# First projections on unnormalised tokens, with a larger pool of raw weight buffers

## The chip, the cores and the metric

The kernel runs on one core of one Trainium2 chip. The metric is the device time of one execution in microseconds (us). PE is the matrix engine, DVE VectorE, ACT ScalarE, POOL GpSimd, SP the engine whose queue issues all the transfers here.

## What is computed

A two-layer encoder over 256 tokens of width 1024, all in fp32. Each layer normalises the tokens, sends them through one wide input projection whose columns feed three mixers (latent attention, convolution, retention) and gates, merges the branches, and adds a normalised result to the tokens; a feed-forward part follows. The part that the change touches is the beginning of layer 0:

```
def rms_norm(x, g):
    y = xf * lax.rsqrt(jnp.mean(xf * xf, -1, keepdims=True) + EPS)
    return y * g
...
    for l in range(DEPTH):
        h = rms_norm(x, ln_mix_pre[l])
        proj = h @ w_in[l]
        c_q, c_kv, k_pe, conv_u, r_q, r_k, r_v, r_g, gate_logits = jnp.split(proj, points, axis=-1)
```

The row factor of the norm is one number for each token and the gain one number for each of the 1024 inputs, so `(x * rs * g) @ w` equals `rs * (x @ (g * w))`. In c_q, c_kv and k_pe (416 columns) lie the latents and the rotary key; r_v are 1024 columns, of which the first 512 are made at the start.

## The kernel before

Tokens lie in two blocks of 128 (b = 0, 1), the 1024 inputs in eight tiles of 128. Every fp32 product is made of three: operands are split into a high part (fp32r) and a low remainder, and high x high, high x low and low x high are summed in a PSUM bank.

**Weights.** `wunit` (L171) takes one unit of 1024 columns a partition: SP transfers it to a raw buffer (tag raw, NRAW = 5 of them), ACT casts it to whi (L175, 9 buffers), DVE subtracts to wlo (L177, 8 buffers). A raw buffer is free when its subtraction is done, and only then may SP issue the transfer that reuses it. SP issues in program order; each transfer also waits for the one eight places ahead of it. `split` (L182, L183) does cast and subtraction for activations.

**Front.** SP brings the gain row (4 KB) and then token block 0. PE runs warm-up matmuls (L128) and spreads the gain row over the partitions by a matmul with ones (L131). `first_norm` (L293) squares a block on ACT and DVE; POOL makes rs (L142, L143); DVE makes hn = x * rs * g (L278); PE transposes hn (L284); `split` writes hT, high and low. Then `behind` multiplies hT by the latents' weights ua (416 columns) and the value weights uv (512): L205 for the products with hT's high part, L208 for those with its low part.

**Behind the front.** `setup_tables` makes sinT, cosT, sinq, cosq from the positions (DVE, then one Sin each on ACT, L365) and the decay constants lg of the retention (27 small DVE operations and one on ACT, L374 to L387). `latent` norms the latents of a block (squares on ACT L457, L458; POOL; DVE L462, L464) and applies the rotary factors to the key (kpad, L392 to L397); later PE transposes cn (L474) and kpad (L475), and ACT copies them to cT and kT. Meanwhile PE runs feature groups, `feat_group` with `mm3` (L186 to L188), for the convolution's inputs; two units of weights each, 24 products for each half j.

**Boundaries.** `boundary` joins two sub-layers, three times in all: the new tokens of block 0 are normed and transposed (L284) while PE still works on block 1's last products, ACT casts hT, and the next sub-layer's products begin.

The order inside an engine is the scheduler's: the program is recorded, and instructions are moved past each other where the data allow it. Loops over units set it only roughly.

## Time and profile before

| | |
|---|---|
| time, median of 3 runs (lowest to highest) | 934.63 us (933.78 to 935.09) |
| the profiled execution, its span | 934.14 us, 932.1 us |
| PE busy | 924.0 us (99%), 4924 matmuls |
| PE weight loads, beside the matmuls | 787.0 us (84%) |
| DVE busy | 694.0 us (74%) |
| ACT busy | 534.6 us (57%) |
| POOL busy | 36.8 us (4%) |
| moved from memory | 164.80 MB, 178 GB/s over the span |

The busy share says how full an engine was over the whole span. The chain says which engine's work, followed back from the end, set it. Busy PE time is modelled and pipelined: a row's duration has a tail that lies under the next row, so the cost of one matmul in a run of equal ones is the distance of their starts. The page's clock row shows the full level over all slices, since records begin with the rise; the level before that is read from the same distances.

### The profile page before, as it was taken

The page shows a single profiled execution, that of the slowest core. Times are in us where ns is not written, and L with a number is a line of the kernel's source. Part 1 is how long each engine was busy: PE and PEld are TensorE (multiplying, and loading weights), DVE is VectorE, ACT ScalarE, POOL GpSimd, SP SyncE. Part 2 cuts the span into 40 slices and gives each one's busy share as a digit, 9 for nine tenths or more (in the row PEclk, how much of TensorE's full clock was granted, in tenths as well). Part 3 has the DMA queues.
Part 4 walks back from the last instruction along what each step waited for, and adds up shares of the span by engine and source line. Part 5 has one row for each costly group of instructions (what it writes and reads, how often), then busy time and mean ns, then how long its engine had stood idle before and what let it go on. Part 6 is the DMA issues. An engine that isn't in the chain of part 4 may idle for free.

```text
span 932.1 us, 13291 instructions
## 1 busy us (share of the span) xinstructions
PE 924.0 (99%) x4924; PEld 787.0 (84%) x4924; DVE 694.0 (74%) x1101; ACT 534.6 (57%) x821; POOL 36.8 (4%) x77
## 2 busy tenths in 40 slices
PE   9999999999999999999999999999999999999997
PEld 6999878888888888888889987788888888888885
DVE  7889999996657766664485899999766677676532
ACT  5774886545545665554365758755454556666421
POOL 2000000000010000000120000010000100000000
PEclk9999999999999999999999999999999999999999
DMA  6885454566636766666376656545665376665621
GB/s 226 250 271 162 139 174 163 154 191 182 193 91 229 248 193 191 189 194 193 102 213 201 182 156 178 183 136 163 197 181 180 126 230 204 186 182 189 201 83 45
DMA packets 113214, 166.70 MB, mean 179 GB/s; under 512 B 5929, under 2 KB 62905, under 8 KB 113150
## 3 DMA queue, kind: packets, MB, share of 16 engines
q1 hardware_dynamic: 113150, 165.87, 58.6%
q8 instruction: 38, 0.62, 0.3%
q14 instruction: 26, 0.21, 0.1%
HBM read 164.80 MB, written 1.05 MB: 178 GB/s over the span
## 4 chain that ended last, share of the span: by engine, by line
PE 97%; DMA 1%; ACT 1%; DVE 0%; SPq 0%; issue 0%; DVEq 0%; POOLq 0%; POOL 0%; ACTq 0%
PE acc L186 20%; PE acc L187 19%; PE acc L188 19%; PE acc L255 13%; PE acc L253 7%; PE acc L205 6%; PE acc L208 3%; PE acc L252 2%; PE tp L627 1%; PE tp L663 1%; PE tp L652 1%; DMA raw<-in_w_in_dram 1%; PE tp L693 1%; PE tp L284 1%; PE tp L187 1%; PE tp L188 1%
## 5 line engine op out<-in xcount | busy, mean ns | idle before, releaser
L177 DVE TENSOR_TENSOR wlo<-raw,whi 128x1024 fp32r<-128x1024 f32 (+1 forms) x300 | 363.3, 1218 | 103.8 <-PE acc L187 58.9
L175 ACT CAST whi<-raw 128x1024 fp32r<-128x1024 f32 (+1 forms) x300 | 312.6, 1049 | 222.8 <-PE acc L188 122.1
L255 PE MATMUL acc<-hT,whi 128*128 128x512 f32 x504 | 179.7, 396 | 0.0
L253 PE MATMUL acc<-hT,wlo 128*128 128x256 f32 x576 | 148.9, 279 | 0.0
L186 PE MATMUL acc<-whi,hT 128*128 128x512 f32 x288 | 118.1, 410 | 0.0
L253 PEld LDWEIGHTS acc<-hT,wlo 128*128 128x128 f32 x576 | 108.6, 189 | 6.2
L187 PE MATMUL acc<-wlo,hT 128*128 128x512 f32 x288 | 112.7, 391 | 0.0
L188 PE MATMUL acc<-whi,hT 128*128 128x512 f32 x288 | 112.5, 391 | 0.0
L255 PEld LDWEIGHTS acc<-hT,whi 128*128 128x128 f32 x504 | 94.6, 188 | 19.5
L535 DVE SCALAR_TENSOR_TENSOR cacc<-apad,ccol,cacc 128x256 f32<-128x256 f32 x240 | 108.8, 482 | 1.3
L186 PE MATMUL acc<-hT,whi 128*128 128x256 f32 x256 | 73.2, 286 | 0.0
L188 PE MATMUL acc<-hT,wlo 128*128 128x256 f32 x256 | 72.4, 283 | 0.0
L187 PE MATMUL acc<-hT,whi 128*128 128x256 f32 x256 | 72.4, 283 | 0.0
L186 PE MATMUL acc<-whi,hidh 128*128 128x512 f32 x176 | 68.6, 390 | 0.0
L187 PE MATMUL acc<-wlo,hidh 128*128 128x512 f32 x176 | 68.5, 389 | 0.0
L188 PE MATMUL acc<-whi,hidl 128*128 128x512 f32 x176 | 68.5, 389 | 0.0
L186 PEld LDWEIGHTS acc<-whi,hT 128*128 128x128 f32 x288 | 54.1, 188 | 13.4 <-issue 3.1
L188 PEld LDWEIGHTS acc<-whi,hT 128*128 128x128 f32 x288 | 54.1, 188 | 12.1
L187 PEld LDWEIGHTS acc<-wlo,hT 128*128 128x128 f32 x288 | 54.2, 188 | 10.2
L205 PE MATMUL acc<-whi,hT 128*128 128x512 f32 (+1 forms) x128 | 49.4, 387 | 0.5 <-ACT hT L182 0.4
L186 PEld LDWEIGHTS acc<-hT,whi 128*128 128x128 f32 x256 | 49.1, 192 | 0.2
L187 PEld LDWEIGHTS acc<-hT,whi 128*128 128x128 f32 x256 | 49.1, 192 | 0.2
(248 smaller groups left out, 1478.6 us busy)
## 6 DMA issues: line engine op xcount, KB each, us to landing
raw<-in_w_in_dram SPq DMA_DIRECT2D x112, 512.0 KB, 4.3
raw<-in_ffn_w_gate_dram SPq DMA_DIRECT2D x44, 512.0 KB, 4.3
raw<-in_ffn_w_up_dram SPq DMA_DIRECT2D x44, 512.0 KB, 4.5
raw<-in_ffn_w_down_dram SPq DMA_DIRECT2D x44, 512.0 KB, 4.5
raw<-in_ret_w_o_dram SPq DMA_DIRECT2D x16, 512.0 KB, 3.5
raw<-in_w_out_dram SPq DMA_DIRECT2D x16, 512.0 KB, 3.6
raw<-in_mla_w_o_dram SPq DMA_DIRECT2D x8, 512.0 KB, 4.7
raw<-in_conv_w_pw_dram SPq DMA_DIRECT2D x8, 512.0 KB, 3.6
```

Of the source, the lines that this page charges most:

```text
L175: S.copy(hi, raw)
L177: V.tensor_sub(lo, raw, hi.bitcast(F32))
L186: T.matmul(o, lh, rh, start=start, stop=False)
L187: T.matmul(o, lh, rl, start=False, stop=False)
L188: T.matmul(o, ll, rh, start=False, stop=stop)
L205: T.matmul(o, ah[:, 2 * i + k, :], w[:, k, :], start=not (i or k or n), stop=False)
L208: T.matmul(o, al[:, 2 * i - 2 + k, :], units[i - 1][0][:, k, :], start=False, stop=i == len(units) and k == 1)
L252: T.matmul(ps, wh, both[:, k, :], start=True, stop=False)
L253: T.matmul(ps[:, SEQ:], wl, both[:, k, :SEQ], start=False, stop=False)
L255: T.matmul(ps, wh, both[:, k, :], start=False, stop=k == KT - 1)
L284: T.transpose(ps[:, j * P:(j + 1) * P], hn[:, (4 * c + j) * P:(4 * c + j + 1) * P], ident)
L535: V.scalar_tensor_tensor(cacc[:, j, :], src, ccol[:, j, w:w + 1], cacc[:, j, :], op0=ALU.mult, op1=ALU.add)
```

## The change

For layer 0 alone, the latents' group and the value group multiply the tokens as they come. PE transposes the raw tokens (`plain_T`), `split` writes uTh and uTl; the gain is put on the weights while they are split (`scaled_unit`, a factor for each partition from pcol, a transposed 8 x 128 gain tile), and the row factor rs on the results (sa for the latents, vrh and vrl for the values). The squares stand behind the latents' weights on ACT and DVE. The normalised hT, which all later groups need, is still made, between the value products. The gain comes as a 512 KB broadcast. A chain (`Line`) fixes the order of the front's instructions on PE, ACT and DVE. NRAW goes from 5 to 7; the warm-ups from 10 to 7 and one; the positions' transfers are issued ahead of the value weights; the decay constants are made behind the rotary queries.

```
-NRAW = 5
-WARM = 10
+NRAW = 7
+WARM = 7
...
-    nc.sync.dma_start(grow1[0:1, :], ln_mix_pre[0:1, :])
     nc.sync.dma_start(xs[:, 0, :], x[0, 0:P, :])
...
+    g8 = act.tile([KT, P], F32, tag="grow", name="g8")
+    nc.sync.dma_start(g8, ln_mix_pre[0].rearrange("(k p) -> k p", p=P))
...
-    for i in range(WARM):
-        T.matmul(pw, warm[:, :P], warm, start=True, stop=True)
-        if i == 3:
-            for c in range(2):
-                T.matmul(gfirst[c], ones, grow1[0:1, c * 512:(c + 1) * 512], start=True, stop=True)
+    keep_busy(WARM)
...
+    def plain_T(b, c, u):
+        ps = tp()
+        for j in range(4):
+            inPE(T.transpose(ps[:, j * P:(j + 1) * P], xs[:, b, (4 * c + j) * P:(4 * c + j + 1) * P], ident))
+        hi, lo = (t[:, 4 * c:4 * c + 4, b * P:(b + 1) * P] for t in u)
+        pv = ps.rearrange("p (j n) -> p j n", j=4)
+        inACT(S.copy(hi, pv))
+        return lambda: inDVE(V.tensor_sub(lo, pv, hi.bitcast(F32)))
+
+    def scaled_unit(src, k0, c, col):
+        raw = wraw(src, 2, c)[:, :2 * c].rearrange("p (k c) -> p k c", k=2)
+        hi, lo = (t[:, :2 * c].rearrange("p (k c) -> p k c", k=2) for t in (hi_tile(), lo_tile()))
+        for k in range(2):
+            inACT(S.activation(hi[:, k, :], raw[:, k, :], AF.Copy, scale=col[:, k0 + k:k0 + k + 1]))
+        for k in range(2):
+            inDVE(V.scalar_tensor_tensor(lo[:, k, :], raw[:, k, :], col[:, k0 + k:k0 + k + 1],
+                                         hi[:, k, :].bitcast(F32), op0=ALU.mult, op1=ALU.subtract))
...
-        S.activation(hn[:, :512], xs[:, b, :512], AF.Square, scale=1.0 / 32.0, accum_out=ss[:, 0:1])
-        V.scalar_tensor_tensor(hn[:, 512:], xs[:, b, 512:], 1.0 / D, xs[:, b, 512:],
-                               op0=ALU.mult, op1=ALU.mult, accum_out=ss[:, 1:2])
-        pre_norm(b, hn, ss, gain, hT)()
+        inACT(S.activation(hn[:, :512], xs[:, b, :512], AF.Square, scale=1.0 / 32.0, accum_out=ss[:, 0:1]))
+        inDVE(V.scalar_tensor_tensor(hn[:, 512:], xs[:, b, 512:], 1.0 / D, xs[:, b, 512:],
+                                     op0=ALU.mult, op1=ALU.mult, accum_out=ss[:, 1:2]))
...
+        lo = plain_T(0, 0, u)
+        lo()
+        unit(0)
+        lo = plain_T(0, 1, u)
+        lo()
+        nc.sync.dma_start(xs[:, 1, :], x[0, P:2 * P, :])
+        keep_busy(1)
+        products(0, 0, "hh")
+        products(0, 0, "lh")
+        for c in range(2):
+            plain_T(1, c, u)()
+        products(0, 0, "hl")
...
+            uT, pcol = fast_first(pas)
+            tables = load_tables()
+            gain = gain_tile(ln_mix_pre[0])
+            squares = [first_squares(b) for b in range(NB)]
+            uv, first = [], []
+            for i in range(4):
+                uv.append(scaled_unit(win[2 * i * P:(2 * i + 2) * P, C_RV:C_RV + 512], 2 * i, 512, pcol))
+                if i < NB:
+                    first.append(pre_norm(i, *squares[i], [gain[:, cs] for cs in halves()], hT, inDVE))
...
+            for b in range(NB):
+                sa = half("sa")[:, :C_CONV]
+                S.activation(sa, pas[b][:, :C_CONV], AF.Copy, scale=first[b].rs)
+                pas[b] = sa
+            for i in range(4):
+                for b in range(NB):
+                    tok_mm(pvs[b], uT, b, 2 * i, uv[i], 2, i == 0, i == 3)
+                if i in (1, 2):
+                    first[i - 1]()
+            for b in range(NB):
+                vh, vl = vrh[:, b, :512], vrl[:, b, :512]
+                S.activation(vh, pvs[b], AF.Copy, scale=first[b].rs)
+                V.scalar_tensor_tensor(vl, pvs[b], first[b].rs, vh.bitcast(F32), op0=ALU.mult, op1=ALU.subtract)
...
+        if l == 0:
+            setup_decays()
```

On PE, at the rotary keys: cn are the normed latents, kpad the rotary keys, the products are those of the feature groups. Before, the first transpose of kpad stands 12 products behind block 0's cn, the second right behind block 1's, in the middle of a group:

```order
L474 MATMUL tp_541<-ident_96,cn_406 128x128 x3
L475 MATMUL tp_541<-ident_96,kpad_109 96x128
L186 MATMUL acc_516<-hT_111,whi_506 128x256
L187 MATMUL acc_516<-hT_111,whi_506 128x256
L188 MATMUL acc_516<-hT_111,wlo_508 128x256
```

And after, 24 products behind block 1's cn, where the next group begins:

```order
L197 MATMUL acc_536<-hT_102,whi_532 128x256
L198 MATMUL acc_536<-hT_102,wlo_534 128x256
L559 MATMUL tp_516<-ident_87,kpad_100 96x128
L196 MATMUL acc_607<-hT_102,whi_597 128x256
L559 MATMUL tp_561<-ident_87,kpad_100 96x128
L197 MATMUL acc_607<-hT_102,whi_597 128x256
L198 MATMUL acc_607<-hT_102,wlo_599 128x256
```

Both transposes of kpad have moved behind the whole second group, around the first product of the third.

On ACT, at the sine tables: whi of 256 and 128 columns are the query weights, of 1024 the feature weights, th the convolution's gate. Before:

```order
L182 CAST vrh<-acc 128x512
L365 ACT_TABLE_LOAD
L365 ACTIVATE sinT<-sinT 128x288
L175 CAST whi<-raw 128x1024 x3
L182 CAST vrh<-acc 128x512
L175 CAST whi<-raw 128x1024 x3
L365 ACTIVATE cosT<-cosT 128x288
L175 CAST whi<-raw 128x1024
L522 ACT_TABLE_LOAD
L522 ACTIVATE th<-acc 128x512
```

And after:

```order
L541 ACTIVATE cn_426,ss2_427<-sa_300 128x256
L542 ACTIVATE cn_426,ss2_427<-sa_300 128x128
L192 CAST whi_726<-raw_724 128x256
L192 CAST whi_722<-raw_724 128x128
L396 ACT_TABLE_LOAD
L396 ACTIVATE sinT_95<-sinT_95 128x288
L192 CAST whi_726<-raw_724 128x256
L192 CAST whi_722<-raw_724 128x128
L192 CAST whi_738<-raw_736 128x256
L192 CAST whi_722<-raw_736 128x128
L618 ACT_TABLE_LOAD
L618 ACTIVATE th_444<-acc_457 128x512
```

The sine has moved behind both blocks' latents and the first query weights, and the gate now stands between sine and cosine (two casts, a table load and the cosine follow), so the tables are loaded twice more.

On ACT, at the first boundary (junk: squares of the banks; hn: squares of the new tokens; whi: weights of the next sub-layer). Before:

```order
L314 ACTIVATE hn,ss_2810<-xs 128x512 x2
L175 CAST whi<-raw 128x1024 x2
L305 ACTIVATE junk,ss_2885<-acc 128x512
L175 CAST whi<-raw 128x1024 x3
L182 CAST hT<-tp 128x4x128 x2
```

And after:

```order
L347 ACTIVATE hn,ss_2858<-xs 128x512 x2
L185 CAST whi<-raw 128x1024 x2
L338 ACTIVATE junk,ss_2933<-acc 128x512
L185 CAST whi<-raw 128x1024 x4
L192 CAST hT<-tp 128x4x128 x2
```

One more weight cast stands ahead of hT's; it is the same at the other two boundaries.

## Rows read from the trace of the kernel before

**Rows 1.** The page, chain that ended last: each engine's share of the span

```profile
PE 97%; DMA 1%; ACT 1%; DVE 0%; SPq 0%; issue 0%; DVEq 0%; POOLq 0%; POOL 0%; ACTq 0%
```

**Rows 2.** Timeline of PE: start and duration (us), line, operation, [idle before <-releaser]

```profile
4.39 3.78 PE L131 MATMUL acc<-grow,ones 1*128 1x512 f32 x4
...
9.36 1.91 PE L284 MATMUL tp<-ident,hn 128*128 128x128 f32 x8
...
11.46 0.72 PE L205 MATMUL acc<-whi,hT 128*128 128x416 f32 x1 [0.19 <-ACT hT L182]
...
12.32 0.55 PE L205 MATMUL acc<-whi,hT 128*128 128x416 f32 x1
12.66 0.47 PE L205 MATMUL acc<-wlo,hT 128*128 128x416 f32 x1
12.97 0.35 PE L205 MATMUL acc<-whi,hT 128*128 128x416 f32 x1
13.16 0.35 PE L205 MATMUL acc<-wlo,hT 128*128 128x416 f32 x1
```

**Rows 3.** Timeline of ScalarE, at the front and at one later boundary

```profile
4.97 0.63 ACT L293 ACTIVATE hn<-xs 128x512 f32<-128x512 f32 x1 [2.97 <-DMA xs<-in_x_dram]
...
5.98 0.88 ACT L175 CAST whi<-raw 128x832 fp32r<-128x832 f32 x1 [0.29 <-DMA raw<-in_w_in_dram]
...
28.88 1.28 ACT L365 ACT_TABLE_LOAD   x1
...
42.07 0.90 ACT L182 CAST whi<-raw 128x256 fp32r<-128x256 f32 x3
...
282.56 1.06 ACT L175 CAST whi<-raw 128x1024 fp32r<-128x1024 f32 x1 [1.19 <-PE tp L284]
```

**Rows 4.** Timeline of SP's queue: issue and duration, transfer

```profile
1.13 0.35 SPq L120 DMA_DIRECT2D xs<-in_x_dram  x1
...
37.03 2.57 SPq L166 DMA_DIRECT2D raw<-in_mla_w_uq_dram  x2
```

**Rows 5.** Timeline of PE: second transposes, last value products, two feature pairs

```profile
14.86 0.60 PE L284 MATMUL tp<-ident,hn 128*128 128x128 f32 x4
...
32.14 1.07 PE L208 MATMUL acc<-whi,hT 128*128 128x512 f32 x4
33.05 0.28 PE L186 MATMUL acc<-hT,whi 128*128 128x256 f32 x1
...
46.12 0.28 PE L186 MATMUL acc<-hT,whi 128*128 128x256 f32 x1
```

**Rows 6.** Timeline of VectorE, from the second norm past kpad

```profile
13.13 1.39 DVE L278 SCALAR_TENSOR_TENSOR hn<-xs,rs,acc 128x512 f32<-128x512 f32 x2
...
21.12 0.16 DVE L348 CAST pos<-pos_i 128x2 f32<-128x2 int32 x1
...
22.53 0.39 DVE L354 TENSOR_SCALAR ang<-inv,pos 128x16 f32<-128x16 f32 x2 [0.67 <-DMA inv<-in_inv_row_dram]
...
25.12 0.17 DVE L374 TENSOR_SCALAR lgt<-lgt 128x16 f32<-128x16 f32 x1 [1.86 <-DMA lgt<-in_ret_decay_logits_dram]
...
40.00 0.17 DVE L384 TENSOR_SCALAR lgt<-lgt 128x16 f32<-128x16 f32 x1
...
40.17 0.17 DVE L397 TENSOR_TENSOR kpad<-kpad,tk 128x16 f32<-128x16 f32 x1
...
44.99 2.35 DVE L177 TENSOR_TENSOR wlo<-raw,whi 128x1024 fp32r<-128x1024 f32 x2
```

**Rows 7.** Groups by line and shape, Pool, first 60 us: busy us, mean ns

```profile
L139 POOL TENSOR_TENSOR rs<-rs,nhalf 128x2 f32<-128x2 f32 x2 | 1.5, 738 | 0.2
```

**Rows 8.** Timeline of PE at two boundaries between sub-layers

```profile
283.55 0.40 PE L188 MATMUL acc<-whi,mTl 128*128 128x512 f32 x1
284.15 0.50 PE L205 MATMUL acc<-whi,hT 128*128 128x512 f32 x1 [0.20 <-ACT hT L182]
...
740.80 0.40 PE L188 MATMUL acc<-whi,mTl 128*128 128x512 f32 x1
741.27 0.50 PE L205 MATMUL acc<-whi,hT 128*128 128x512 f32 x1
```

More of the change, by code (lines that the diff above doesn't have):

```diff
@@ L117, in tile_hybrid_encoder, with __init__, __call__ @@
     xs = cst.tile([P, NB, D], F32, tag="xs", name="xs")
-    grow1 = mid("grow1")
-    nc.sync.dma_start(grow1[0:1, :], ln_mix_pre[0:1, :])
     nc.sync.dma_start(xs[:, 0, :], x[0, 0:P, :])
-    ones = cst.tile([1, P], F32, tag="ones", name="ones")
-    V.memset(ones, 1.0)
+    g8 = act.tile([KT, P], F32, tag="grow", name="g8")
+    nc.sync.dma_start(g8, ln_mix_pre[0].rearrange("(k p) -> k p", p=P))
+    class Line:
+        def __init__(self):
+            self.last = None
+        def __call__(self, ins):
+            if self.last is not None:
+                tc.add_manual_dep(ins.ins, self.last, mybir.DependencyInfo(
+                    mybir.DependencyClass.NoSync, mybir.DependencyReason.DATA), reason="order")
+            self.last = ins.ins.name
+    inPE, inACT, inDVE = Line(), Line(), Line()
     warm = act.tile([P, 512], BF16, tag="half", name="warm", bufs=7)
@@ L125, in tile_hybrid_encoder, with keep_busy @@
     pw = tp()
-    gfirst = [acc() for _ in range(2)]
-    for i in range(WARM):
-        T.matmul(pw, warm[:, :P], warm, start=True, stop=True)
-        if i == 3:
-            for c in range(2):
-                T.matmul(gfirst[c], ones, grow1[0:1, c * 512:(c + 1) * 512], start=True, stop=True)
+    def keep_busy(n):
+        for _ in range(n):
+            inPE(T.matmul(pw, warm[:, :P], warm, start=True, stop=True))
+    keep_busy(WARM)
     ident = cst.tile([P, P], F32, tag="ident", name="ident")
@@ L272, in new_hT, with pre_norm @@
         return t[:, :, :SEQ], t[:, :, SEQ:]
-    def pre_norm(b, hn, ss, gain, hT):
+    def pre_norm(b, hn, ss, gain, hT, line=lambda ins: None):
         rs = sm.tile([P, 1], F32, tag="rs", name="rs")
@@ L277, in pre_norm @@
         for c, cs in enumerate(halves()):
-            V.scalar_tensor_tensor(hn[:, cs], xs[:, b, cs], rs, gain[c], op0=ALU.mult, op1=ALU.mult)
+            line(V.scalar_tensor_tensor(hn[:, cs], xs[:, b, cs], rs, gain[c], op0=ALU.mult, op1=ALU.mult))
         def transposes():
@@ L368, in setup_tables, with setup_decays @@
         V.tensor_scalar(sinq, sinr, sc, None, op0=ALU.mult)
+    def setup_decays():
+        lgt = half("lgt")
+        n = DEPTH * 2 * RH
+        xl = lgt[:, 0:n]
+        nc.sync.dma_start(xl, ret_decay_logits.rearrange("l t h -> (l t h)").partition_broadcast(P))
+        nc.sync.dma_start(relt, rel)
         u = lgt[:, 16:32]
@@ L404, in a_unit, with fast_first, unit, products @@
         return wunit(win[2 * i * P:(2 * i + 2) * P, C_A:C_CONV], 2, C_CONV)
-    first_norm(0, gfirst, hT)
-    ua = [a_unit(w_in[0], i) for i in range(2)]
-    nc.sync.dma_start(xs[:, 1, :], x[0, P:2 * P, :])
-    first_norm(1, gfirst, hT)
+    def fast_first(pas):
+        pg = tp()
+        inPE(T.transpose(pg[:, :KT], g8, ident[:KT, :KT]))
+        col = act.tile([P, KT], F32, tag="gcol", name="pcol")
+        inDVE(V.tensor_copy(col, pg[:, :KT]))
+        u = [big(n, F32R).rearrange("p (k n) -> p k n", k=KT) for n in ("uTh", "uTl")]
+        units = []
+        def unit(i):
+            units.append(scaled_unit(w_in[0][2 * i * P:(2 * i + 2) * P, C_A:C_CONV], 2 * i, C_CONV, col))
+        def products(i, b, what):
+            o = pas[b][:, :C_CONV]
+            for k in range(2):
+                t = u[what == "lh"][:, 2 * i + k, b * P:(b + 1) * P]
+                inPE(T.matmul(o, t, units[i][what == "hl"][:, k, :], start=i == 0 and k == 0 and what == "hh",
+                              stop=i == 3 and k == 1 and what == "hl"))
+        lo = plain_T(0, 0, u)
[10 more added lines that the diff above has]
+        products(0, 0, "hl")
+        for what in ("hh", "lh", "hl"):
+            products(0, 1, what)
+        for i in range(1, 4):
+            unit(i)
+            for b in range(NB):
+                for what in ("hh", "lh"):
+                    products(i, b, what)
+            for b in range(NB):
+                products(i, b, "hl")
+        return u, col
@@ L410, in tile_hybrid_encoder @@
     for l in range(DEPTH):
         win = w_in[l]
+        pas = [acc() for _ in range(NB)]
+        pvs = [acc() for _ in range(NB)]
         if l == 0:
-            ua += [a_unit(win, i) for i in range(2, 4)]
+            uT, pcol = fast_first(pas)
[7 more added lines that the diff above has]
+                    first.append(pre_norm(i, *squares[i], [gain[:, cs] for cs in halves()], hT, inDVE))
@@ L416, in tile_hybrid_encoder @@
         else:
             ua = [a_unit(win, i) for i in range(4)]
-        uv = [wunit(win[2 * i * P:(2 * i + 2) * P, C_RV:C_RV + 512], 2, 512) for i in range(4)]
+            uv = [wunit(win[2 * i * P:(2 * i + 2) * P, C_RV:C_RV + 512], 2, 512) for i in range(4)]
         gqkv = half("gqkv")[:, :QR + KVR]
@@ L607, in tile_hybrid_encoder @@
         pe_steps.append(qpe_T)
+        if l == 0:
+            setup_decays()
         for g in range(2):
```

28 lines of the change are left out of this document (14 added, 14 removed).

## The prediction, made before the changed kernel ran

> **What bounds the kernel now.** I read the page's chain first: PE is 97% of the chain that ended last [rows 1]. So PE is packed, and the change can gain or lose at three kinds of place only: the front up to the first real product, the products behind it that run at the slow clock, and any new or old wait of PE. Then PE's own timeline at the front [rows 2]: behind the warm-ups and the matmuls that spread the gains, eight transposes from 9.36, the first product at 11.46. Two products of 416 columns start 0.34 apart at 12.32 and 12.66, the next pair 0.19 apart at 12.97 and 13.16: up to 12.9 PE ran at the lower of its two levels (1.2 GHz), from there at 2.4. Last, the timelines of VectorE and ScalarE in the first 46 us, and PE's two later idle pieces.
>
> About 0.2% (1.87 us) is what a measurement of this kernel can tell from no change. The profiled execution took 934.14 (its span 932.1 and 2.04 around it); the median of the three runs is 934.63, 0.49 higher. I sum against 934.14.
>
> **The first product.** Before, ScalarE's squares begin when the tokens have landed, at 4.97 [rows 3], and squares, norm, multiplication by the gain, transposes and casts lie between that and 11.46. After, the tokens are the first transfer and not the second, one issue earlier (an issue takes 0.35, I take 0.4 [rows 4]), and PE transposes them raw. Nine transposes at the low clock, 0.22 each (eight take 1.91 with a tail [rows 2]): 4.8 to 6.7. Behind the first four, ScalarE copies (0.6) and scales the first weights; a scaled half of 416 columns is about 0.64 (832 take 0.88 [rows 3], so half with its fixed part is near 0.54, and 0.1 for the scale by a column). First product: about 7.2, 4.3 earlier.
>
> **The clock.** It rose 3.5 us after the eight transposes had begun and 1.4 after the first product [rows 2]. The same distances in the new front give 4.8 + 3.5 = 8.3 and 7.2 + 1.4 = 8.6; I take 8.5. Bounds: 6, since warm-ups, transposes and products now follow each other with one gap of 0.5; and 12.9, where it rose before.
>
> **PE up to the feature groups.** From 7.2: 4 products at 0.35 (1.40), 44 at 0.187 (8.23), the eight transposes of the second token block at 0.11 (0.88; four take 0.60 with a tail of 0.27 [rows 5]), and 0.6 for casts that PE waits for between the first products: 18.3. Then 48 products of 512 columns at 0.227 (10.90; four take 0.91 up to 33.05 [rows 5]) and sixteen more transposes, those of the normalised tokens (1.74): 31.0. Before, this point was 33.05 [rows 5]. So far -2.05. The gain matmuls and the three warm-ups that go away stood ahead of the first product and count only through its time.
>
> **The new wait: kpad.** Before, the transposes of the rotary keys stood with the latents', and PE did not wait for them. After, they stand behind more of the feature groups, at the place that PE reached at 46.12 [rows 5]. PE gets there 46.12 - 33.05 - 0.25 (the two transposes, since moved behind it) = 12.8 after 31.0, at 43.8. When is kpad ready? VectorE, step by step. Before, from the first position cast (21.12) to the last addition of block 0 (40.17), 19.05 us go by; 2.53 of it are two waits (0.67 and 1.86) and 20 are small decay operations, first at 25.12 and last at 40.00 [rows 6], some 0.09 each once pipelined (1.8). Both leave: 14.7. New in that stretch: the low parts of the normalised hT, four of 512 columns at 0.6 (2.4), two more subtractions of feature weights at 1.13 (2.3; two take 2.35 with a tail [rows 6]), four small ones (0.3): 19.7. Ahead of it, from the low parts of the second block at 10.1: those two at 0.6, six scaled subtractions of 416 columns at 0.57, two squares at 0.70, eight subtractions of 512 and four multiplications for hn at 0.66 (two take 1.39 with a tail of 0.7 [rows 6]): 14.0, so 24.1. Sum 43.8, if VectorE never waits. It will: the latents' squares go through ScalarE and Pool (its power takes 0.74 [rows 7]) before VectorE can scale them, twice, and sinq now waits for a sine behind a table load of 1.28 [rows 3]; by these durations 1.4 in all. kpad comes at 45.2, and PE waits 1.4 (bounds 0, if every hand-over is covered, and 2.0). I take 1.4, since VectorE's list has no gap that could swallow it. The group behind begins at 45.5 against 46.12: the front is worth **-0.6**. From here on PE's list is the old one, so the 0.6 reaches the end.
>
> **Two more table loads.** The order on ScalarE is now sine, tanh, sine, tanh: 2 x 1.28 more, beside PE's products. The one that reaches PE is that ahead of sinq, counted above; the second sine's feeds cosq, which VectorE needs 5 us later, behind two subtractions.
>
> **Seven raw buffers.** PE waits for no weight transfer, so by themselves they give nothing. At two of the three later boundaries PE idles: 283.55 to 284.15 and 740.80 to 741.27, less a step of 0.23, 0.37 and 0.24 [rows 8]. At the first a weight cast that began late, at 282.56 [rows 3], stood ahead of hT's. Casts now find their weights two transfers earlier, but four stand ahead of hT's, not three; the fourth needs a buffer that the last product before the transposes frees, 0.9 before that late cast began, so it is out at 282.7, hT's first half is there at 283.3, and PE wants it at 283.8: **-0.6** for the two. If the fourth cast runs one cast behind that late start, hT comes 0.96 later instead: +0.96 twice and 0.2 at the third boundary, which bounds this term at +2.1.
>
> **The rest.** The decays go between the convolution's taps on VectorE, 22 operations of 0.1 with some 20 us of other work around them; SP issues their transfer between two weight transfers and waits for nothing there. The positions' transfers move ahead of the value weights, 0.4 us of issuing each, while the queue's landings are what limits those. All this costs nothing on PE while the weights lead by a unit; without that lead, 0.5.
>
> **Sum:** 934.14 - 0.6 - 0.6 = 932.9.
>
> **Rivals.**
> *No kpad wait.* If VectorE's hand-overs are hidden, kpad is there with PE at 43.8: 934.14 - 2.0 - 0.6 = 931.5. For it: the additive list ends just when PE arrives. Against: the squares and the sine stand behind casts on ScalarE, in a list with no slack.
> *The clock rises late.* If transposes do not raise it and it rises at 12.9 again, products from 8.5 to 12.9 run at 0.35: 4.4 x (1 - 0.187/0.35) = 2.05 more, 0.45 of it cover for waits, and kpad moves with PE: the front is +1.0, the total 934.5. Against it: before, the clock rose with 1.9 us of transposes just behind it [rows 2], when the warm-ups and gain matmuls ahead of them had not raised it.
> The Trainium skill ("TensorE: Matmul & The Clock Gate", Part 4: PE-mode transpose) says that a transpose does not count as busy in the same way and that the full clock does not engage for it; by that rule this rival holds, and the trace speaks rather against it.
> *Slower: the sine behind the query weights.* On ScalarE the sine's table load stands behind two casts of the query up-projection's weights. Before, their transfers were issued from 37.03 and the first casts ran at 42.07 [rows 3, 4]. After, I expect the weights by 33, 3.5 before ScalarE asks. If they came at 42 again, the load, the sine, sinq and all that stands behind it on VectorE, kpad too, would be 5 us later: 938. It decides from about 37 on, a us for each us. Against it: with seven buffers the transfer waits for an earlier slot, near 29.
> *No effect.* The front gains and a wait that I don't see gives it back: 934.1 to 934.6.
>
> **How the numbers follow.** Forecast 0.47, its own range 932.2 to 933.8 (the clock between 6 and 10, the kpad wait 0.8 to 1.6), two fifths of it below 932.76, the bound for faster. No kpad wait 0.25, late clock 0.15, slower 0.08, no effect 0.05. Faster by over 0.2%: 0.25 + 0.19 = 0.44. Slower: 0.08. Within: 0.48. The range 931.2 to 935.2 leaves out the slower rival, the worse half of the boundary term's bad end and the best of the first rival.
>
> **What would show it.** First product near 7.2 and products 0.19 apart from about 8.5; the first feature product near 31.0; one wait of PE at the kpad transposes, 1.4, released by VectorE; no idle at the two boundaries. It is wrong if products stay 0.35 apart beyond 10, if PE waits for the first casts by more than 1 us, or if the kpad wait exceeds 2.

## The result, and the profile after

The changed kernel takes 940.38 us (median of six runs, 939.90 to 942.55), the kernel before 935.10 on the same chip (six runs, 933.78 to 937.21). The ratio is 1.0061, 95% interval [1.0050, 1.0073]: slower by 0.6%, where 932.9 was forecast. The profiled execution took 940.2 with a span of 938.3; before, 934.14 and 932.1. The medians lie 5.3 us apart, the two profiled executions 6.1, and the last products in their traces 6.3; the account below is of these 6.3.

The chain on the page, which answers to [rows 1]:

```profile
PE 94%; DMA 2%; DVE 2%; ACT 1%; issue 0%; SPq 0%; POOL 0%; DVEq 0%; POOLq 0%; ACTq 0%
```

PE is still nearly the whole chain, so the 6.3 us are PE's, as idle time or as a slower pace. The list of PE's waits (engine, tile and line, what released it: us in total, times, longest) shows the idle time:

```profile
PE tp L140 <- POOL warm L135: 1.3, 1, 1.3
PE tp L559 <- DVE kpad L435: 1.1, 1, 1.1
PE acc L197 <- DVE hT L193: 0.9, 1, 0.9
PE acc L218 <- DVE hT L193: 0.3, 1, 0.3
PE acc L196 <- ACT hT L192: 0.3, 1, 0.3
```

The first wait stands ahead of the first warm-up and is old. The others are new, and the forecast had only the second. The one of L218 lies at 474 us, behind the boundary between the layers; the other three lie in the front. PE's timeline there (start, duration, line, operation, idle time before and its releaser), against [rows 2, 5]:

```profile
4.60 1.97 PE L306 MATMUL tp<-ident,xs 128*128 128x128 f32 x8
6.36 0.43 PE L140 MATMUL tp<-warm 128*128 128x512 bf16 x1
6.93 0.99 PE L460 MATMUL acc<-whi,uTh 128*128 128x416 f32 x2
7.76 0.54 PE L460 MATMUL acc<-whi,uTl 128*128 128x416 f32 x2
8.28 1.09 PE L306 MATMUL tp<-ident,xs 128*128 128x128 f32 x8
...
31.43 0.38 PE L196 MATMUL acc<-hT,whi 128*128 128x256 f32 x1 [0.28 <-ACT hT L192]
32.73 0.38 PE L197 MATMUL acc<-hT,whi 128*128 128x256 f32 x1 [0.92 <-DVE hT L193]
...
46.78 0.31 PE L559 MATMUL tp<-ident,kpad 128*96 128x128 f32 x1 [1.05 <-DVE kpad L435]
46.85 0.36 PE L196 MATMUL acc<-hT,whi 128*128 128x256 f32 x1
```

The first product comes at 6.93. Eight transposes take 1.97 at 4.60 and 1.09 at 8.28: the first eight ran at the lower level of the clock (0.21 apart up to 6.15), and the two products of the row at 7.76 already stand 0.19 apart, as the products at the upper level did before. So the clock rose in between; the trace's own clock record begins at 6.45. The first feature product is at 31.43, 1.6 us ahead of [rows 5]. Then 1.2 go in two waits for the second block's normalised rows and 1.05 in the one for kpad, and the new front is 0.9 us behind the old. What these waits go back to, on ScalarE (first row) and VectorE:

```profile
16.59 5.20 ACT L317 ACTIVATE whi<-raw,pcol 128x512 fp32r<-128x512 f32 x8 [2.12 <-DMA raw<-in_w_in_dram]
17.35 1.42 DVE L319 SCALAR_TENSOR_TENSOR wlo<-raw,pcol,whi 128x512 fp32r<-128x512 f32 x2 [1.87 <-ACT whi L317]
25.31 0.16 DVE L379 CAST pos<-pos_i 128x2 f32<-128x2 int32 x1
31.10 0.48 DVE L546 SCALAR_TENSOR_TENSOR cn<-sa,rs,gqkv 128x256 f32<-128x256 f32 x1 [1.00 <-POOL rs L149]
31.99 1.28 DVE L193 TENSOR_TENSOR hT<-tp,hT 128x512 fp32r<-128x512 f32 x2
46.73 0.17 DVE L435 TENSOR_TENSOR kpad<-kpad,tk 128x16 f32<-128x16 f32 x1
```

That is 0.9 of 6.3. For the rest I set each product of one trace beside the same product of the other and read how the distance between them grows. It shrinks by 0.35 up to 190 us; then it grows by 1.26 from 190 to 283, by 1.70 from 400 to 469, by 1.25 from 640 to 741 and by 1.75 from 860 to the end, 6.0 in all and evenly within each stretch. The boundaries between take 0.47 and 0.34 off and put 0.58 on. The stretches are those in which the stationary operand is the retention's, the convolution's, the merged or the hidden rows. Hidden-row products of the kernel before, the first number of each row the start:

```profile
440.12 0.39 PE L187 MATMUL acc<-wlo,hidh 128*128 128x512 f32 x1
440.35 0.39 PE L188 MATMUL acc<-whi,hidl 128*128 128x512 f32 x1
440.58 0.39 PE L186 MATMUL acc<-whi,hidh 128*128 128x512 f32 x1
440.80 0.39 PE L187 MATMUL acc<-wlo,hidh 128*128 128x512 f32 x1
```

and of the changed one:

```profile
440.08 0.40 PE L196 MATMUL acc<-whi,hidh 128*128 128x512 f32 x1
440.31 0.40 PE L197 MATMUL acc<-wlo,hidh 128*128 128x512 f32 x1
440.55 0.40 PE L198 MATMUL acc<-whi,hidl 128*128 128x512 f32 x1
440.78 0.40 PE L196 MATMUL acc<-whi,hidh 128*128 128x512 f32 x1
```

Three steps take 0.68 before and 0.70 after. Over the 524 such steps (of up to 260 ns) in each trace the mean is 226.7 ns before and 233.3 after: nobody waits, and the granted clock is 1.00 in both. PE's busy time by stretch counts the same thing (its length, PE busy, instructions, granted clock, DMA share, GB/s). Before and after, 440 to 460 us:

```profile
440.00:460.00 20.00, 20.00 (x90) 1.00 0.32 92
```

```profile
440.00:460.00 20.00, 20.00 (x88) 1.00 0.43 122
```

### The profile page after: what moved, and what is told of

It reads as the page before. It is cut to its first block, busy times and chain, and to the rows that moved or that the text cites. A ratio compares the mean times of both kernels' runs of the same rounds, so it can differ in the third digit from the quotient of the medians.

```text
span 938.3 us, 13337 instructions
## 1 busy us (share of the span) xinstructions
PE 927.9 (99%) x4935; PEld 786.6 (84%) x4935; DVE 697.6 (74%) x1113; ACT 541.8 (58%) x837; POOL 36.0 (4%) x77
## 3 DMA queue, kind: packets, MB, share of 16 engines
HBM read 165.32 MB, written 1.05 MB: 177 GB/s over the span
## 4 chain that ended last, share of the span: by engine, by line
PE 94%; DMA 2%; DVE 2%; ACT 1%; issue 0%; SPq 0%; POOL 0%; DVEq 0%; POOLq 0%; ACTq 0%
PE acc L196 20%; PE acc L197 19%; PE acc L198 19%; PE acc L265 13%; PE acc L263 7%; PE acc L215 4%; PE acc L218 2%; DMA raw<-in_w_in_dram 2%; PE acc L262 2%; PE tp L726 1%; PE tp L762 1%; PE tp L751 1%; PE tp L792 1%; DVE wlo L187 1%; PE tp L197 0%; PE tp L196 0%
## 5 line engine op out<-in xcount | busy, mean ns | idle before, releaser
L187 DVE TENSOR_TENSOR wlo<-raw,whi 128x1024 fp32r<-128x1024 f32 (+1 forms) x292 | 354.3, 1219 | 100.4 <-PE acc L197 63.0
L185 ACT CAST whi<-raw 128x1024 fp32r<-128x1024 f32 (+1 forms) x292 | 304.6, 1051 | 211.0 <-PE acc L198 131.4
L263 PEld LDWEIGHTS acc<-hT,wlo 128*128 128x128 f32 x576 | 108.7, 189 | 6.2
L198 PEld LDWEIGHTS acc<-hT,wlo 128*128 128x128 f32 x256 | 49.1, 192 | 0.0
```

The costliest lines, as they stand in the source:

```text
L185: S.copy(hi, raw)
L187: V.tensor_sub(lo, raw, hi.bitcast(F32))
L198: T.matmul(o, ll, rh, start=False, stop=stop)
L263: T.matmul(ps[:, SEQ:], wl, both[:, k, :SEQ], start=False, stop=False)
```

## The experiments

**What the slow pace hangs on.** The diff gives one thing that these late products share: `col = act.tile([P, KT], F32, tag="gcol")` now stands ahead of the allocation of the large tiles (`big`). It is 32 bytes wide. In the kernel before, the large tiles begin at multiples of 512 bytes in each partition; in the changed one the first of them begins at byte 144,928, 32 beyond such a multiple, and so do all behind it. The changed program also has a smaller descriptor scratch, a reserved stretch ahead of all tiles (`dynamic_dma_scratch_size=1024`, an edit that the section on the change does not name). First the changed kernel with this tile twice as wide:

```diff
-        col = act.tile([P, KT], F32, tag="gcol", name="pcol")
+        col = act.tile([P, 16], F32, tag="gcol", name="pcol")
```

> The changed kernel, but the tile for the gain column (pcol, later gcol) is 16 columns wide and not 8, so that it takes 64 bytes of each partition and not 32. In the changed kernel the tiles allocated behind it (the hidden activations, the merged tokens, the retention's outputs) start 32 bytes past a multiple of 64; here all of them start at a multiple of 64. No instruction is added, removed or moved. Theory A (the address): products with these tiles, which start 0.231 to 0.236 apart in the changed kernel, return to 0.227, and the 5.3 us that the trace shows spread evenly over these stretches go away: about 934.7, near the kernel before. Theory B (the pace is slower because of what runs beside PE, seven raw buffers and earlier transfers among it): nothing changes, 940.2.

941.44, ratio 1.0072 [1.0054, 1.0090]: no gain, mean step 233.3 ns. Either 64 bytes aren't enough, or the theory is wrong. So the kernel before was given the shift alone, with a tile that nothing uses:

```diff
+        if l == 0:
+            act.tile([P, 8], F32, tag="shim", name="shim")
```

> The kernel before, with one unused tile of 32 bytes allocated ahead of the tiles for hidden activations, merged tokens and retention outputs; these then start 32 bytes past a multiple of 64, the instructions are the same. Theory A (the address): products with these tiles start 0.231 to 0.236 apart instead of 0.227 and the time is about 5 us longer, 939 to 940. Theory B (neighbouring work): no change, 934 to 935.

940.39, ratio 1.0057 [1.0039, 1.0075]. No instruction differs from the kernel before, and the front ends where it did (0.04 later at 52 us), but the last products are 5.3 us late. This shows that the place of the tiles alone costs nearly all of what the changed kernel loses. The same with `[P, 16]`, 64 bytes:

> As the run before it, with an unused tile of 64 bytes: the same tiles are shifted, but start at multiples of 64. Theory A in its form 'alignment to 64 bytes' expects no change against the kernel before (934 to 935); in its form 'any shift, by the distance between tiles or banks' it expects some of the 5 us (936 to 940). Theory B: no change.

940.15, 1.0053 [1.0038, 1.0068]. Then with `[P, 32]` and `[P, 64]`, 128 and 256 bytes (with the smaller descriptor scratch, for room):

> The kernel before with an unused tile of 128 bytes ahead of the token, mixed and hidden rows' tiles, and the smaller scratch: they begin 128 bytes behind a multiple of 512. With 256 bytes the time was that of the kernel before, with 64 it was 5 us more. If 128 bytes are enough: 935 and 0.227 us apart; if it has to be 256: 940 and 0.230 to 0.236.

> The kernel before with an unused tile of 256 bytes ahead of the same tiles (and the smaller descriptor scratch, which makes the room). If a multiple of 256 is enough, the products stay 0.227 us apart and the time stays at 935. If it has to be 512, the pace falls to 0.230 to 0.236 as with 32 and 64 bytes, and the time is 940.

128 bytes: 941.86, 1.0071 [1.0053, 1.0089]. 256 bytes: 935.66, 1.0003 [0.9994, 1.0012]. The stretch from 440 to 460 us, first 128, then 256:

```profile
440.00:460.00 20.00, 20.00 (x87) 1.00 0.42 131
```

```profile
440.00:460.00 20.00, 20.00 (x90) 1.00 0.35 109
```

So on these tiles a multiple of 256 bytes keeps the pace, and offsets of 32, 64 and 128 lose it. The 256-byte run has the smaller scratch too and keeps the pace, so the scratch is not the cause. Last, the changed kernel with its column tile 512 bytes wide (`[P, 128]`):

> The changed kernel with the column tile made 512 bytes wide instead of 32, so that the tiles behind it (tokens, mixed rows, hidden rows) begin at a multiple of 512 bytes again, as in the kernel before; nothing else moves. Theory of the addresses, with the multiple that matters at 512: products from these tiles start 0.227 us apart instead of 0.233, the 5.3 us spread over the program go, and what is left is the front (+0.9 at the first transposes of the key tile) and the boundaries (about 0): 935 to 936 us, 0.1% above the kernel before at most. Rival, the slow pace comes with something else that the change does (seven raw buffers, the smaller scratch, more traffic in the front): the pace stays at 0.233 and the time at 940.

935.08 against 935.22, ratio 1.0000 [0.9991, 1.0008]: the 0.6% is gone. The mean step over each trace, in ns, for products of 512 columns that follow one another (steps over 260 left out):

| stationary operand | steps before | before | after | 32 B | 64 B | 128 B | 256 B | after, 512 B | weights 32 B |
|---|---|---|---|---|---|---|---|---|---|
| hidden rows | 524 | 226.7 | 233.3 | 233.3 | 233.3 | 232.4 | 226.7 | 226.7 | 233.3 |
| merged rows | 178 | 227.9 | 233.0 | 233.2 | 233.3 | 232.4 | 227.9 | 228.0 | 233.1 |
| retention rows | 184 | 227.7 | 233.0 | 233.1 | 233.3 | 232.4 | 227.7 | 227.7 | 233.1 |
| convolution rows | 96 | 226.7 | 233.1 | 233.1 | 233.3 | 232.8 | 226.7 | 226.7 | 233.3 |
| hT (not moved) | 1049 | 228.6 | 228.6 | 228.7 | 228.8 | 228.8 | 228.7 | 228.8 | 233.1 |

524 x 6.6, 178 x 5.1, 184 x 5.3 and 96 x 6.4 ns make 6.0 us, what the four stretches lost. hT lies outside the shifted tiles and keeps its pace. A sixth group, the attention's rows (82 steps), goes from 230.7 to 232.9, so a place at the multiple does not bring every group to 226.7. The last column is the other operand: the kernel before with only the weight tiles 32 bytes off.

```diff
+    act.tile([P, 120], F32, tag="shim2", name="shim2")
     grow1 = mid("grow1")
...
+    wp.tile([P, 8], F32, tag="shim", name="shim", bufs=1)
     vec_steps = []
```

> The kernel before with an unused tile of 32 bytes ahead of the weight tiles (raw, whi, wlo) and one of 480 bytes behind them (and the smaller scratch for room): the weights begin 32 bytes behind a multiple of 512, every other tile keeps its place against 512. The products of the long token groups have the weights as moving operand and the tokens, mixed or hidden rows as stationary one; the feature groups and the doubled groups of the feed-forward stage have it the other way round. Theory, the place of the stationary operand sets the pace: the products of hidden rows at 430 to 465 us stay 0.227 us apart, those with stationary weights slow down, and the time rises by some us. Rival, the moving operand's place sets it: the hidden-row products fall to 0.233. Rival, only the token, mixed and hidden tiles matter: no change, 935.

947.24 against 936.01, 1.0130 [1.0110, 1.0151]. The first theory named here falls: the stationary operands lie at their old places, and the products still take 233 ns, the hT products too. It is enough that one operand, the 128 stationary columns or the 512 moving ones, begins off the multiple while the other does not. No run moves both by the same distance, so whether each one's own place counts or the distance between the two is open. The doubled groups, which hold the weights stationary, lose only 0.7 us in the 100 us from 300 to 400; their step is 232.6 with every tile in place. Why these are slow anyway was not tried.

**What seven raw buffers do.** The 64-byte version with five of them:

```diff
-NRAW = 7
+NRAW = 5
```

> The changed kernel with the 64-byte gain column and with five raw weight buffers as before. It tells what the seven buffers are worth by themselves. If they remove PE's idle time at the first and last boundary (0.37 and 0.24 in the kernel before), these come back here: 0.5 us more than the aligned kernel with seven, 935.2; the front may lose some tenths more, since the value weights' transfers then wait for subtractions. If transfers were in each other's way with seven, it is faster than with seven, below 934.5.

943.02, 1.0080 [1.0062, 1.0098], beside 941.44 with seven. In its profile PE waits 2.2 us for kpad and not 1.1, and stands 2.9 us further back at 52 us. But each of the two profiles also holds a stretch at half the clock, granted 0.50 from 49 to 52 us with five and from 8 to 11 us with seven, and single runs of the two overlap (940.81 to 943.76 and 940.21 to 942.86). That the new front needs the buffers is likely, not shown. The other way round, the kernel before with seven:

> The kernel before with seven raw weight buffers instead of five and the smaller scratch, all tiles at the multiples of 512 bytes that they had. The front is the old one. The prediction's step: buffers alone do nothing in the front and give back 0.3 and 0.2 us at the boundaries at 284 and 741 us: 934.5 to 935. Rival, they also bring the loss of 0.5 us at 468 to 471 us: 935.1, no difference. Rival to the theory of the addresses, the smaller scratch or the further apart raw buffers slow the pace by themselves: 940.

935.83, 1.0004 [0.9996, 1.0013]. At 284 and 741 us it gains 0.48 and 0.36, of which 0.17 and 0.13 are lost again within 4 us; at 471 it loses 0.88. So the buffers alone bring the gains and the loss. In the changed kernel the gains have a second possible cause: the kernel before with the 32-byte shift, which has five buffers, gains 0.46 and 0.26 at the same two places, since its slower products come later to the normalised rows and no longer wait for them. The loss it does not have. The cause of the loss stands in VectorE's timeline; first the kernel before, then the changed kernel, whose time here is 3 us later:

```profile
466.55 3.29 DVE L177 TENSOR_TENSOR wlo<-raw,whi 128x832 fp32r<-128x832 f32 x3
469.75 1.28 DVE L183 TENSOR_TENSOR hT<-tp,hT 128x512 fp32r<-128x512 f32 x2
```

```profile
469.34 4.42 DVE L187 TENSOR_TENSOR wlo<-raw,whi 128x832 fp32r<-128x832 f32 x4
473.68 1.28 DVE L193 TENSOR_TENSOR hT<-tp,hT 128x512 fp32r<-128x512 f32 x2
```

Four weight subtractions stand ahead of hT's; before, three did, in 3.29. With the subtractions from the third value unit on held behind hT's, in the aligned kernel, that is the changed one with the 512-byte column tile (`after` adds the dependency on the subtraction of hT that was noted under this name):

```diff
-            uv = [wunit(win[2 * i * P:(2 * i + 2) * P, C_RV:C_RV + 512], 2, 512) for i in range(4)]
+            uv = [wunit(win[2 * i * P:(2 * i + 2) * P, C_RV:C_RV + 512], 2, 512,
+                        vecs="lonext" if i >= 2 else None) for i in range(4)]
...
-        V.tensor_sub(lo, raw, hi.bitcast(F32))
+        after(V.tensor_sub(lo, raw, hi.bitcast(F32)), vecs)
```

> The aligned changed kernel with one dependency more: at the boundary between the layers VectorE makes the third value unit's subtraction behind the two of the first block's normalised rows instead of ahead of them. Theory: the loss at 470 us (0.85 us against the kernel before) comes from this subtraction, which seven raw buffers let in early; it goes, and the time is 934.2 to 934.8, 0.1% under the kernel before. Rival: the wait is set by ScalarE's cast of these rows or by the normalisation itself, and stays.

934.59 against 936.01, 0.9985 [0.9976, 0.9994], and VectorE's rows are

```profile
467.72 3.29 DVE L193 TENSOR_TENSOR wlo<-raw,whi 128x832 fp32r<-128x832 f32 x3
470.92 1.28 DVE L304 TENSOR_TENSOR hT<-tp,hT 128x512 fp32r<-128x512 f32 x2
472.12 1.22 DVE L193 TENSOR_TENSOR wlo<-raw,whi 128x1024 fp32r<-128x1024 f32 x1
```

The step of 0.88 at 471 us is gone (1.18 behind the kernel before on both sides of it). That cause is shown.

**The front.** Its waits were first attacked by order. Casts and subtractions of the second feature unit held behind those of the second block's hT:

```diff
+        behind_hT = len(units_made) == 1
+        units_made.append(n)
+        hold = (inACT, inDVE) if behind_hT else (lambda ins: None,) * 2
-        S.copy(hi, raw)
+        hold[0](S.copy(hi, raw))
...
-        V.tensor_sub(lo, raw, hi.bitcast(F32))
+        hold[1](V.tensor_sub(lo, raw, hi.bitcast(F32)))
```

> The aligned changed kernel with one more edit: on ScalarE and VectorE the cast and the subtraction of the second feature unit's weights are held behind the two casts and subtractions of the second block's normalised rows. Theory: the first feature product found these rows late because the feature casts stood ahead of them, so the two waits of 0.3 and 0.9 us at 31.4 and 32.7 us go; the positions and the tables move too, and the wait for the key tile (1.05) stays or shrinks by as much as its chain comes earlier: 933 to 935 us. Rival: PE runs into the held second unit instead (its subtraction now stands behind the value rows on VectorE), and the wait only changes its name: no gain over the aligned kernel.

936.54, 1.0019 [1.0007, 1.0031]: worse. In its profile (939.66, 3.1 above the median) the hT wait went, and waits of 1.6 for weights and 2.6 for kpad came, since the position casts fell behind hT as well. Then, on top of the mended third boundary, only the third feature unit's cast, the first latents' squares and their scaling held, and the key tile's transposes put later:

```diff
+            hold = "first1" if l == 0 and b == 0 else ""
-            S.activation(cn[:, :QR], pa[:, :QR], AF.Square, scale=1.0 / 16.0, accum_out=ss[:, 0:1])
+            after(S.activation(cn[:, :QR], pa[:, :QR], AF.Square, scale=1.0 / 16.0, accum_out=ss[:, 0:1]), "hi" + hold)
...
-        for b in range(NB):
-            pe_steps.append(latent(pas[b], b))
+        lat = [latent(pas[b], b) for b in range(NB)]
+        pe_steps.extend(lat)
+        if l == 0:
+            pe_steps.extend([nop] + [f.key for f in lat])
```

> The same with two more edits in the front: ScalarE makes the squares of the first latent block and the third feature unit's cast behind the casts of the second block's normalised rows, VectorE the latent rows' scaling behind their subtractions; and the transposes of the key tile stand one and two half groups later on PE, each in a bank of its own. Theory: the two waits for the normalised rows (0.3 and 1.1 us in the aligned kernel) and the one for the key tile (1.0) go, and the front ends 1.5 to 2.4 us earlier than in the aligned kernel: 932 to 933. Rival: the waits move to the feature weights' subtractions or the latent transposes, which now stand later: 934.5 to 936.

934.17 against 936.01, 0.9986 [0.9976, 0.9997], no better than the 0.9985 without these edits. The waits for hT and kpad went, and one of 1.7 came for the fourth feature unit's subtraction, which now stood behind the cosine's work. With the cosine's work made to follow that subtraction, and the key tile later, but the old order ahead of hT:

```diff
+            cos_first = V.scalar_tensor_tensor(dst, tv, -TWO_PI_1, av, op0=ALU.mult, op1=ALU.add)
-            V.scalar_tensor_tensor(dst, tv, -TWO_PI_1, av, op0=ALU.mult, op1=ALU.add)
...
+            if len(made) == 4:
+                held["f3"] = sub.ins.name
+                after(ahead.pop(), "f3")
```

> The aligned changed kernel with the third boundary's order mended and the key tile's transposes one and two half groups later (and the fourth feature unit's subtraction kept ahead of the cosine's reduction), value weights as in the changed kernel. Theory: the wait of 1.0 us for the key tile goes, the waits of 1.4 for the second block's normalised rows stay: 933.4 to 934.2. Rival: the normalised rows' wait grows or PE meets the next group's weights late by the same 1 us: 934.5.

934.23 against 934.35, 0.9999 [0.9990, 1.0007]. The kpad wait is gone; that for hT (0.8) and one for weights (0.5) remain. Then the transfers. The first value unit's ahead of the tables', with the gain's falling behind all four:

```diff
-            tables = load_tables()
-            gain = gain_tile(ln_mix_pre[0])
             squares = [first_squares(b) for b in range(NB)]
...
+                if i == 0:
+                    gain = gain_tile(ln_mix_pre[0])
+                    tables = load_tables()
```

> The aligned changed kernel with the third boundary's order mended (as the run with the third value unit held), and the first value unit's transfer ahead of those of the positions, the tables and the gain; the gain's comes behind all four value units. With it the schedule puts the second block's normalised rows ahead of the latent rows' scaling on VectorE. Theory, late value weights made the front late: ScalarE's and VectorE's waits of 1.8 and 1.6 us for them shrink to under 0.5, the whole chain behind comes about 1 us earlier, the key tile is ready at 45.4 to 45.7 and the time is 933.3 to 934.3. Rival, the order of the queues is what counts: the waits move on (the gain's transfer now ends later, the fourth feature unit's subtraction stands behind the sine work), and the time stays at 934.5 to 935.5.

937.57, 1.0033 [1.0021, 1.0045]. A new wait, of VectorE, answers in part why:

```profile
21.58 1.42 DVE L294 SCALAR_TENSOR_TENSOR hn<-xs,rs,gain 128x512 f32<-128x512 f32 x2 [3.12 <-DMA gain<-in_ln_mix_pre_dram]
```

With the key tile later and the fourth feature unit ahead of the cosine as well:

> The same with two more edits: the key tile's transposes one and two half groups later on PE, in banks of their own, and the fourth feature unit's subtraction ahead of the cosine's reduction on VectorE (it cost a wait of 1.7 us in the run that reordered the front). Theory, the order of the queues and the key tile's place set the front: all waits of PE between 30 and 50 us together under 0.6 us, the front 2 us earlier than in the aligned kernel, 932 to 933.2. Rival, the first weights' landing or another wait takes their place: 934 or more.

936.37, 1.0017 [1.0008, 1.0025]; the gain is waited for there too, 5.3 us, and PE waits 3.1 for a value unit behind it. In that wait the granted clock falls to the lower level; PE's busy time by stretch, in the form used above:

```profile
24.00:30.00 6.00, 5.52 (x15) 0.50 1.03 334
```

Value products start 0.43 us apart there and 0.23 from 31 us on, so the loss is the wait and what the clock adds to it. The run without the two edits has stretches at 0.50 too, from 8 to 11 us, behind a wait of PE of 1.7 for the first scaled weights, and at 45.2 to 48.6. So gain and values first, tables last, on the kernel with the key tile later:

```diff
-            tables = load_tables()
             gain = gain_tile(ln_mix_pre[0])
...
+                if i == 3:
+                    tables = load_tables()
```

> The kernel of the run with the key tile later, with one change on the transfer queue: gain and the four value units are issued ahead of the positions and tables instead of behind them; the order on the compute engines stays. Theory, the value weights land late because they are issued behind the tables: ScalarE's wait for them (1.7 us in two waits) goes, the first feature product and the normalised rows come 0.5 to 1 us earlier, the time is 933.3 to 934. Rival, the transfers themselves fill the queue at that time: the wait stays and so does the time, 934.2.

933.89 against 934.76, 0.9991 [0.9982, 1.0000]. ScalarE's wait for the value weights, 0.7 in that kernel's profile, went, but the one for the first feature unit rose from 2.8 to 4.4, and the first feature product stayed where it was (31.48 against 31.50). The late value weights are not what holds the front, then; the next transfer is as late. The first two feature units ahead of five small transfers, four rows for the convolution and the retention's gain row:

```diff
+        if l == 0:
+            early.append([wunit(win[k0 * P:(k0 + 4) * P, C_CONV + CH:C_CONV + CH + 256], 4, 256) for k0 in (0, 4)])
+        prow, grow = load_rows()
```

> The same with the first two feature units' transfers ahead of the convolution's and the gain column's rows, and their casts and subtractions where they land. Theory: ScalarE's wait of 2.8 us for the first feature unit goes, the second block's normalised rows come out ahead of the first feature product, PE's waits for them (0.8 to 1.4 us) go, the front ends 1.5 to 2 us ahead of the aligned kernel's and the time is 932 to 933. Rival: the feature casts now stand ahead of the latent rows' evacuation, and the latent transposes or the key tile come late instead: 934 or more.

932.18 against 934.76, 0.9975 [0.9965, 0.9986]: faster than both kernels, than the kernel before by 0.25%. The wait list of PE:

```profile
PE tp L140 <- POOL warm L135: 1.3, 1, 1.3
PE tp L590 <- DVE kpad L453: 0.8, 1, 0.8
PE acc L478 <- ACT whi L334: 0.2, 1, 0.2
```

The first feature product runs at 30.62 without a wait, 2.4 ahead of the kernel before, and behind kpad PE is still 1.4 ahead. At 52 us it is 2.0 ahead of the run with gain and values first and tables last. But 0.79 of that is there at the first product already (6.93 and 7.72), by when the first weights landed; PE's waits behind the first product are 1.1 and 0.5 there and 0.8 here. The casts of the second block's rows on ScalarE, first the changed kernel, then this one:

```profile
28.20 1.05 ACT L185 CAST whi<-raw 128x1024 fp32r<-128x1024 f32 x1 [0.26 <-DMA raw<-in_w_in_dram]
...
29.86 1.03 ACT L185 CAST whi<-raw 128x1024 fp32r<-128x1024 f32 x1
30.80 1.06 ACT L192 CAST hT<-tp 128x512 fp32r<-128x512 f32 x2
```

```profile
27.71 1.05 ACT L194 CAST whi<-raw 128x1024 fp32r<-128x1024 f32 x1 [0.23 <-DVE ang L402]
28.67 1.06 ACT L313 CAST hT<-tp 128x512 fp32r<-128x512 f32 x2
```

One profile is one draw of the front, though: PE's wait for the first scaled weights (L460 in the changed kernel) ranged from nothing to 2.1 us over the profiles of these versions, by when the first transfers landed. In the five profiles where it was longest (1.5 to 2.1 us: 64-byte tile, second feature unit held, third value unit held, first latents held, first value unit ahead) the granted clock was at 0.50 for a stretch right behind it, from 9 to 11.9 us for example with the third value unit held; in the others it stayed at 1.00 there. So late first weights cost twice in these profiles. The front's numbers are good to a microsecond or two, the ratios average over that.

## Why the prediction was wrong

Forecast -1.2 us, measured at the last products of the two profiles +6.3.

- **First product 7.2, clock 8.5:** the product came at 6.93. The clock rose earlier than forecast, between 6.15 and 7.76 (6.45 by the record), 1.9 behind the start of the transposes and ahead of the first product; neither of the two distances carried over from the old front (3.5 and 1.4). The rival of the late clock (12.9) fell. The Trainium skill's rule that it went with ("TensorE: Matmul & The Clock Gate", Part 4: PE-mode transpose) isn't refuted by that: from 4.40 to 6.36 PE ran only transposes and the clock rose right behind, but the warm-ups stood ahead of them, and in the profile of the 512-byte version the record begins at 4.65, when the first of the eight transposes had just begun. This case can't test it alone.
- **First feature product 31.0:** 31.43. 0.3 of the difference is the pace: 48 value products at 233 and not 227 ns, from the shifted token tiles. With these in place it was 30.95.
- **PE at kpad 43.8:** 45.57 (the last product at 45.45 plus its 0.12). This step failed. It counted products and transposes behind 31.0 and no wait; the 1.2 us for hT's second block was not in the sum. I had put hT's subtractions into VectorE's list as work, but had not asked when PE wants them, nor what ScalarE casts ahead of them. ScalarE's own list, as made for VectorE, would have shown three feature casts and the latents' squares there; and on VectorE the latents' scaling (31.10), which waits 1.00 for POOL, stands ahead of the subtraction at 31.99.
- **kpad ready 45.2, wait 1.4:** ready near 46.7, wait 1.05. The wait was well sized only because both ends were late. The step that failed is the start of VectorE's list: the position cast was put at 24.1 and ran at 25.31, since VectorE waited 1.87 for value weights at 17.35, and ScalarE 2.12 for their transfer, which the text took for hidden ("while the queue's landings are what limits those"). The four issues put ahead of that transfer ran from 4.27 to 7.53, 3.3 us and not 1.6. From the position cast to block 0's last addition it took 21.25 (25.31 to 46.56), with the forecast at 21.1.
- **Front -0.6:** +0.9.
- **Boundaries -0.6:** two gained, 0.47 and 0.34, but the slower products alone give 0.46 and 0.26 there; the buffers alone, with the pace kept, leave 0.31 and 0.20. The third lost 0.58. It was named, as part of a bad end of the term (ScalarE's fourth cast); the engine that did it was VectorE, with its fourth subtraction.
- **"The rest ... costs nothing on PE":** this is the step that decided it, with "From here on PE's list is the old one, so the 0.6 reaches the end". The list was the old one, its pace was not. The new column tile is in the diff, and 8 floats were read as no cost, because only instructions were counted. It moved the large tiles by 32 bytes, and products on them lost 5 to 7 ns each, 6.0 us. No forecast case held it: the slower rival (the sine behind the query weights) is another mechanism, and its 938 is another time.

Without that term the changed kernel ties (1.0000 [0.9991, 1.0008]), which the range 931.2 to 935.2 held (935.08). With the third boundary's order, the key tile's place and the order of the transfers mended as well it gains 0.25%.

## What to carry to other kernels

When a diff adds, drops or resizes a tile in a pool, list where every tile behind it begins, before and after: a small tile in front can slow each matmul that reads a large one. A loss spread evenly over many products with no wait is found by putting the same products of two traces beside each other. And for a front that is packed again, make the list of every engine that feeds PE, with the landing of each transfer, not that of the one engine that ends last; and read the granted clock behind each wait of PE before two fronts are compared by one profile each.

## What was not expected of the hardware

Products with a 128x128 stationary operand and 512 moving columns of 4 bytes start 226.7 to 228.8 ns apart (means by group; 230.7 for the attention's rows) when both operands' tiles begin at a multiple of 256 bytes in the partition, and 232.4 to 233.3 when one of them begins 32, 64 or 128 bytes beyond it (the moving one was tried at 32 only). At 32 bytes both cost alike (233.3 each on hidden rows). On products of 256 moving columns no such loss was seen: where one follows another in the feature groups the mean step is 119.4 ns in the kernel before and 118.2 with their weights shifted (820 steps). The doubled groups run at 232.6 with all tiles in place. The Trainium skill ("SBUF — State Buffer", Operand start alignment) asks that an operand start at a multiple of its element size; every shifted tile here does (4 bytes), so that rule is kept in all these runs while the pace differs. What in the memory or the engine makes this difference stays open.
